# The gate projection by seven products, another order of the seven, and an earlier start of ACT in a two-layer hybrid decoder trunk

## The chip, the cores and the metric

One core of one Trainium2 chip. The time is device microseconds of one execution, the median of 3 runs. Five engines work beside each other, each through its own list of instructions in order: PE (matrix products; PEld is its loading of weights), DVE (elementwise), ACT (elementwise with function tables), POOL (elementwise) and SP, which here only issues transfers from memory. They wait for each other through semaphores.

## The reference

Two layers over 512 tokens of width 1024, all float32, then a last RMSNorm. In each layer the part that this change touches is the feed-forward:

```python
def swiglu(h, w_gate, w_up, w_down):
    return (jax.nn.silu(h @ w_gate) * (h @ w_up)) @ w_down
# in each layer: h = h + hybrid_mixer(rmsnorm(h, ...), w_in, ...)
#                h = h + swiglu(rmsnorm(h, norm_ffn), w_gate, w_up, w_down)
# h: 512 x 1024, w_gate and w_up: 1024 x 2816, w_down: 2816 x 1024
```

The mixer ahead of it (one input projection, dilated attention, Mamba-2 scan, one output projection) is as before, but for the very first product of layer 0: it multiplies the normalised x by 512 columns of w_in.

## The kernel before, in words

The kernel keeps everything transposed: channels on the 128 partitions, the 512 tokens along the free side. hT[0] to hT[7] hold the residual stream.

**Products at full accuracy.** Every float32 operand is split in two fp32r parts, high and low: ACT casts the high part, DVE subtracts to get the low one (split_x for activations, split_w for weights). A product is three matmuls: high x high, high x low, low x high. The split weights live in rings of three buffers each (tags whi and wlo, NWH = 3), each of 128 x 1024: eight 128x128 blocks. Raw weights arrive in chunks of 1 MB in two buffers (tag raw, NRAW = 2): 1024 rows by 256 columns, so two blocks of output channels, a pair.

**The feed-forward.** Its 22 blocks of 128 hidden channels are done in four parts of 6, 6, 6 and 4 (PARTS), so 3, 3, 3 and 2 pairs. A part makes its gate and up blocks, and then its share of the down projection, which adds to hT block by block (eight blocks of 6 x 3 matmuls in a part of six). In the first part of each layer gate and up are plain: block() issues 8 x 3 matmuls of 512 columns for each block. In the other three parts (eight pairs in each layer) the gate blocks are plain and the up pair goes through seven() (line 1114).

**seven().** It computes a 2 x 2 block product (two halves of the 1024 channels, two blocks of outputs, two halves of the 512 tokens) with seven half-size products in place of eight, after Strassen and Winograd. The weight sides of the seven are: two quarters of the raw chunk as they are (tile a, products a0 and aK), one more quarter (tile d, half a buffer), and four sums of quarters, s[0] to s[3], that DVE makes in a tile called wsum (two buffers): s[0] and s[1] are split into tile b, s[2] and s[3] into tile c. Each product is 4 x 3 matmuls of 256 columns. The activation sides (X: b, t12, t34) are made once for a layer in normed(). Before, the seven run in the order a0, aK, bK, b0, c0, cK, d; all four sums are written before b is split, and as the planner counts dependences by tile, the split of b waits for the last of them. DVE (and one copy on ACT) recombine the products in PSUM into two outputs, m and o.

**Who sets the order.** Operations are collected in a Plan with a cost and a due time (at(...), clock[0]), and Plan.schedule places them on the engines by due time, as buffers allow; the result is a fixed list of instructions for each engine. `LEAD` = 14 lets splits and sums be placed up to 14 us ahead of their first product.

**The start (from line 468).** SP issues pmix (8 KB of norm weights), then hT[0], w0[0], hT[1], w0[1] and so on. PE multiplies a tile of ones nine times meanwhile. For each k, ACT scales hT[k] (xh), squares hT[k] for the norm, and casts w0[k]; DVE makes the low parts. ACT's first instruction is a load of its function table, placed behind its wait for hT[0].

Of the kernel before, what the change touches and what calls it, by code (L numbers as in the profile page):

```python
# [15 lines left out]
ALU = mybir.AluOpType  # L16
# [24 lines left out]
E_XW = 'dve'  # L41
RES_G = 6
NEAR_G = 6.0
GATE7 = 0
PARTS = (6, 6, 6, 4)
HH = S // 2
KQ = KD // 2
# [132 lines left out]
class VTile:  # L180


    def __init__(self, pool, shape, dtype, tag, name, space):
        self.pool, self.shape, self.dtype, self.tag, self.name = pool, shape, dtype, tag, name
        self.psum = space
        self.ap = None
        self.writer, self.readers, self.uses = None, [], 0
        self.live = False

    def get(self):  # L190
        if self.ap is None:
            kw = {} if self.tag is None else {"tag": self.tag[0], "bufs": self.tag[1]}
            self.ap = self.pool.tile(self.shape, self.dtype, name=self.name, **kw)
        return self.ap


class Op:
# [6 lines left out]
class Plan:  # L204
# [4 lines left out]
    def add(self, eng, dur, outs, ins, fn, prio=None, table=None, lat=0.0):  # L209
        o = Op()  # L210
        o.eng, o.dur, o.lat, o.fn, o.table = eng, dur, lat, fn, table
        o.prio = self.t if prio is None else prio
        o.n, o.users = len(self.ops), []
        deps = set()
        outs = [v.tile for v in outs]
        ins = [v.tile for v in ins if isinstance(v, View)]
        for t in ins:
            assert t.writer is not None, f"{t.name} is read before it is written"
            deps.add(t.writer)
        for t in outs:  # L220
            if t.writer is not None:
                deps.add(t.writer)
            deps.update(t.readers)
        for t in ins:
            t.readers.append(o)
        for t in outs:
            t.writer, t.readers = o, []
        deps.discard(o)
        o.tiles = list({id(t): t for t in outs + ins}.values())
        for t in o.tiles:  # L230
            t.uses += 1
        o.deps = deps
        for d in deps:
            d.users.append(o)
        self.ops.append(o)
        return o
# [107 lines left out]
def hybrid_trunk(  # L344
# [24 lines left out]
    def C(shape, name, dt=F32):  # L369
        n = nm(name)  # L370
        return View(VTile(cp, shape, dt, None, n, False), shape)

    def G(name, dt=F32):
        return new(gp, [P, S], dt, ("g", NG), name)

    def big(name, dt=F32):
        return new(wp, [P, 4 * S], dt, ("big", 2), name)
# [13 lines left out]
    def R(v):  # L391
        return v.real() if isinstance(v, View) else v

    def at(t):
        plan.t = t
# [9 lines left out]
    def tt(eng, o, a, b, alu):  # L405
        plan.add(eng, dcost(eng, o, [a, b]), [o], [a, b],
                 lambda: ENG[eng].tensor_tensor(R(o), R(a), R(b), alu))  # L407
# [18 lines left out]
    def memset(eng, o, val):  # L426
        plan.add(eng, 0.1 + 0.9e-3 * o.free, [o], [], lambda: ENG[eng].memset(R(o), val))

    TABLE = {AF.Exp: "exp", AF.Ln: "ln", AF.Silu: "silu", AF.Sin: "silu"}

    def act(o, a, func, scale=None, bias=None, accum=None):
        ptr = [s for s in (scale, bias) if isinstance(s, View)]
        outs = [o] + ([accum] if accum is not None else [])

        def fn():
            kw = {}
            if scale is not None:
                kw["scale"] = R(scale)
            if bias is not None:
                kw["bias"] = R(bias)  # L440
            if accum is not None:
                kw["accum_out"] = R(accum)
            if func == AF.Copy and not kw:
                nc.scalar.copy(R(o), R(a))  # L444
            else:
                nc.scalar.activation(R(o), R(a), func, **kw)  # L446
        cost = 0.83e-3 * o.free + (0.053 if a.tile.psum else 0.093) + 0.093 * len(ptr)
        plan.add("act", cost, outs, [a] + ptr, fn, table=TABLE.get(func))

    def mms(outs, prods, each, prio=None):  # L450

# [7 lines left out]
                    nc.tensor.matmul(R(p[0]), R(p[1]), R(p[2]), start=p[3], stop=p[4])  # L459
        plan.add("pe", each * len(prods), outs, ins, fn, prio, lat=0.08)  # L460

    def load(o, src, kb):
        plan.add("sp", max(0.47, kb / 351.0), [o], [], lambda: nc.sync.dma_start(R(o), src), lat=2.0)

    def tposes(t, parts, name=None):
        mms([t], parts, 0.108)


    at(-40.0)
    pmix = C([P, 16], "pmix")  # L470
    load(pmix, columns[:, PC_MIX:PC_MIX + 16], 8)
    hT = [C([P, S], f"hT{k}") for k in range(KD)]

    raw0 = []
    for k in range(KD):
        load(hT[k], xT[k * P:(k + 1) * P, :], 256)
        raw0.append(G("w0"))
        load(raw0[k], w_in[0, k * P:(k + 1) * P, XBC_COL + 1024:XBC_COL + 1024 + S], 256)
    at(-35.0)
    ones = C([P, P], "ones")  # L480
    memset("pool", ones, 1.0)

    t = tr()
    mms([t], [(t[:, 0:P], ones, ones, True, True)] * 9, 0.43)
    nhalf = C([P, NT], "nhalf")
    memset("pool", nhalf, -0.5)

# [63 lines left out]
    class Norm:  # L551
# [2 lines left out]
        def __init__(self, n):  # L554
            self.n, self.ss, self.row = n, None, None

        def square(self, tl, eng="dve"):
            s = G("sq")
            act(s, tl, AF.Square)
            if self.ss is None:  # L560
                self.ss = s
            else:
                tt(eng, self.ss, self.ss, s, ALU.add)
# [31 lines left out]
    for k in range(KD):  # L595
        at(-20.0 + k)
        xs_next.append(split_x(hT[k], pmix[:, k:k + 1]))
        wh, wl = split_x(raw0[k], None)
        for j, t in enumerate(first):
            js = slice(j * P, (j + 1) * P)  # L600
            xh, xl = xs_next[k]
            mms([t], [(t, wh[:, js], xh, k == 0, False), (t, wh[:, js], xl, False, False),
                      (t, wl[:, js], xh, False, k == KD - 1)], 0.2165, clock[0])
            clock[0] += 3 * 0.2165
        at(-12.0 + k)
        norm_next.square(hT[k])


    at(-12.0)
# [504 lines left out]
    def seven(ids, X):  # L1114
        raw = whl[ids[0]][0]
        q = [[raw[:, j * KQ:(j + 1) * KQ, i * P:(i + 1) * P] for j in range(2)] for i in range(2)]
        at(clock[0] - LEAD)

        def split(src, nk=KD):
            hi, lo = new(wp, [P, 8, P], F32R, ("whi", NWH), "whi"), new(wp, [P, 8, P], F32R, ("wlo", NWH), "wlo")  # L1120
            copy("act", hi[:, 0:nk, :], src)
            tt("dve", lo[:, 0:nk, :], src, hi[:, 0:nk, :].bitcast(F32), ALU.subtract)
            return hi, lo
        a = split(raw[:, :, 0:P])
        sm = big("wsum").rearrange("p (k c) -> p k c", c=P)
        s = [sm[:, i * KQ:(i + 1) * KQ, :] for i in range(4)]
        tt("dve", s[0], q[1][0], q[1][1], ALU.add)
        tt("dve", s[1], s[0], q[0][0], ALU.add)
        tt("dve", s[2], q[0][0], q[1][0], ALU.add)
        tt("dve", s[3], q[0][1], s[1], ALU.add)  # L1130
        b = split(sm[:, 0:KD, :])
        c = split(sm[:, KD:, :])
        d = split(q[1][1], KQ)
        t1_, t2_ = slice(0, HH), slice(HH, S)

        def prod(o, w, k0, xs, half):
            hi, lo = w
            for ka in range(0, KQ, 2):
                pr = []
                for k in (ka, ka + 1):  # L1140
                    xh, xl = (v[:, half] for v in xs[k])
                    for i, (wv, v) in enumerate(((hi, xh), (hi, xl), (lo, xh))):
                        pr.append((o, wv[:, k0 + k, :], v, k == 0 and i == 0, k == KQ - 1 and i == 2))
                mms([o], pr, 0.1175, clock[0])
                clock[0] += len(pr) * 0.1175
            at(clock[0] - 6.0)

        def bcast(v):
            return v.unsqueeze(1).broadcast_to([P, 2, HH])

        def halves(v):
            return v.rearrange("p (u c) -> p u c", u=2)

        b1, b2 = X["b"][0:KQ], X["b"][KQ:]
        p17, p26 = hold(), acc()
        e, m, o = G("e"), G("m"), G("o")
        prod(p17[:, 0:HH], a, 0, b1, t1_)
        copy("act", e[:, 0:HH], p17[:, 0:HH])
        prod(p26[:, 0:HH], a, KQ, b2, t1_)
        prod(p26[:, HH:], b, KQ, X["t12"], t2_)  # L1160
        tt("dve", halves(m), halves(p26), bcast(e[:, 0:HH]), ALU.add)
        p45, p3 = acc(), tr()
        prod(p45[:, HH:], b, 0, X["t12"], t1_)
        prod(p17[:, HH:], c, 0, X["t34"], t1_)
        tt("dve", e[:, HH:], p17[:, HH:], m[:, HH:], ALU.add)
        prod(p3[:, 0:HH], c, KQ, b2, t2_)
        tt("dve", m[:, HH:], m[:, HH:], p3[:, 0:HH], ALU.add)
        tt("dve", m[:, HH:], m[:, HH:], p45[:, HH:], ALU.add)
        prod(p45[:, 0:HH], d, 0, X["t34"], t2_)
        tt("dve", halves(o), halves(p45), bcast(e[:, HH:]), ALU.add)  # L1170
        at(clock[0] - 4.0)
        return m, o

# [100 lines left out]
```

## Time and profile before

| | us |
|---|---|
| median of 3 runs | 1323.34 (1321.87 to 1323.98) |
| the profiled execution | 1324.0 |
| its span, first to last instruction | 1322.2 |
| PE busy in the span | 1294.6 (98%) |
| DVE busy | 905.7 (68%) |
| ACT busy | 653.0 (49%) |
| POOL busy | 140.2 (11%) |
| mean granted clock of PE | 0.995 |

The profiled execution gives durations; its own time is 1.8 us above its span and 0.7 us above the median of the runs. Busy shares are means over stages of different kinds: attention and scan keep DVE, ACT and POOL busy, the feed-forward hardly touches POOL. The feed-forward of layer 0 lies at about 275 to 670 us, that of layer 1 at about 928 to 1297 us.

### The profile page before, as it was taken

Reading aid. Unit: us, or ns where it says so; the run is one execution under the profiler, and the core shown is the slowest. Engines: PE = TensorE matmul, PEld = TensorE weight load, DVE = VectorE, ACT = ScalarE, POOL = GpSimd, SP = SyncE. Lnnn points to the kernel's source line nnn. Section 1 sums busy time; section 2 is a strip of 40 time slices with the busy share of each in tenths; the row PEclk is TensorE's granted clock in tenths of the full one; section 3 lists DMA queues with packets and bytes.
Section 4 is the critical chain, followed back from the end, with each engine's and each line's share of the span. In section 5 each row is a group of like instructions: output and inputs, shape, how many; then the busy total and the mean of one; then the engine's idle time right before and its main releaser. Section 6 shows DMA issues by size and latency. Waiting matters only on the chain.

```text
span 1322.2 us, 17020 instructions
## 1 busy us (share of the span) xinstructions
PE 1294.6 (98%) x6674; PEld 1067.4 (81%) x6674; DVE 905.7 (68%) x1510; ACT 653.0 (49%) x1029; POOL 140.2 (11%) x109
## 2 busy tenths in 40 slices
PE   8999998999999999999999999999999999999997
PEld 7877776778888888888888777767888889888896
DVE  6987779768746555555779687887786456465464
ACT  7677656656323323323647687466553233243253
POOL 0014455000000000000000234620000000000000
PEclk9999999999999999999999999999999999999999
DMA  7222211123232233233332222111332332322421
GB/s 242 64 64 64 64 65 64 33 80 102 90 112 96 69 123 99 78 112 96 96 98 65 94 66 65 56 40 45 88 112 84 119 96 72 120 96 73 135 96 63
DMA packets 105727, 115.57 MB, mean 87 GB/s; under 512 B 4656, under 2 KB 95024, under 8 KB 105648
## 3 DMA queue, kind: packets, MB, share of 16 engines
q1 hardware_dynamic: 105648, 114.49, 27.4%
q8 instruction: 52, 0.85, 0.3%
q14 instruction: 27, 0.22, 0.1%
HBM read 112.39 MB, written 2.10 MB: 87 GB/s over the span
## 4 chain that ended last, share of the span: by engine, by line
PE 87%; DVE 7%; ACT 2%; POOL 2%; issue 1%; DMA 0%; POOLq 0%; SPq 0%; DVEq 0%; ACTq 0%
PE acc L459 72%; PE hold L459 7%; PE tr L459 6%; PE tr L457 3%; DVE wlo L407 2%; DVE qs L407 1%; POOL xbc L407 1%; DVE xbc L418 1%; POOL qr L407 1%; ACT whi L444 1%; DVE wsum L407 0%; DVE qs L921 0%; POOL qs L407 0%; ACT L446 0%; DVE sa L413 0%
## 5 line engine op out<-in xcount | busy, mean ns | idle before, releaser
L459 PE MATMUL acc<-xh,whi 128*128 128x512 f32 (+1 forms) x1552 | 588.4, 379 | 1.4 <-DVE o L407 0.9
L459 PE MATMUL acc<-xl,whi 128*128 128x512 f32 (+1 forms) x1552 | 579.4, 373 | 0.0
L459 PE MATMUL acc<-xh,wlo 128*128 128x512 f32 (+1 forms) x1536 | 573.3, 373 | 4.2 <-DVE wlo L407 4.2
L444 ACT CAST whi<-raw 128x1024 fp32r<-128x1024 f32 (+3 forms) x248 | 212.4, 859 | 335.2 <-PE acc L459 303.0
L459 PEld LDWEIGHTS acc<-xh,whi 128*128 128x128 f32 x1552 | 293.2, 189 | 55.1 <-issue 5.6
L459 PEld LDWEIGHTS acc<-xh,wlo 128*128 128x128 f32 x1536 | 289.7, 189 | 58.6 <-DVE wlo L407 6.7
L459 PEld LDWEIGHTS acc<-xl,whi 128*128 128x128 f32 x1552 | 293.3, 189 | 47.1 <-issue 0.5
L407 DVE TENSOR_TENSOR wlo<-raw,whi 128x1024 fp32r<-128x1024 f32 (+2 forms) x240 | 246.8, 1030 | 27.6 <-ACT whi L444 27.3
L407 DVE TENSOR_TENSOR hT<-hT,acc 128x512 f32<-128x512 f32 x104 | 71.1, 685 | 103.6 <-PE acc L459 102.9
L407 DVE TENSOR_TENSOR wlo<-wsum,whi 128x1024 fp32r<-128x1024 f32 x32 | 39.0, 1224 | 88.4 <-ACT whi L444 88.4
L573 POOL TENSOR_TENSOR rcol<-var,nhalf 128x4 f32<-128x4 f32 x8 | 8.7, 1089 | 577.2 <-DVE var L413 577.2
L446 ACT ACT_TABLE_LOAD x49 | 62.9, 1283 | 6.6 <-DMA hT<-in_xT_dram 4.1
L444 ACT CAST whi<-wsum 128x1024 fp32r<-128x1024 f32 x32 | 33.5, 1048 | 53.9 <-PE acc L459 46.3
L418 DVE SCALAR_TENSOR_TENSOR xbc<-cu,prm,xbc 128x511 f32<-128x511 f32 (+2 forms) x72 | 58.4, 819 | 0.8
L444 ACT CAST xh<-ga 128x512 fp32r<-128x512 f32 x44 | 27.3, 621 | 54.5 <-DVE ga L407 38.6
L446 ACT ACTIVATE sa<-sa,mx 128x512 f32<-128x512 f32 (+3 forms) x64 | 36.0, 562 | 36.5 <-DVE mx L979 36.2
L1230 POOL TENSOR_TENSOR fr<-fvar,nhalf 128x1 f32<-128x1 f32 x4 | 2.2, 546 | 353.5 <-DVE fvar L413 353.5
L979 DVE CUSTOM_DVE_ANT_0 sa<-tr,cst 128x512 f32<-128x512 f32 (+3 forms) x64 | 30.7, 479 | 10.3 <-PE tr L459 10.2
L459 PE MATMUL hold<-xh,wlo 128*128 128x256 f32 x128 | 36.3, 284 | 0.0
L459 PE MATMUL hold<-xl,whi 128*128 128x256 f32 x128 | 36.2, 283 | 0.0
L459 PE MATMUL hold<-xh,whi 128*128 128x256 f32 x128 | 36.1, 282 | 0.0
L407 DVE TENSOR_TENSOR xl<-ga,xh 128x512 fp32r<-128x512 f32 x44 | 30.3, 688 | 8.3 <-ACT xh L444 8.2
(216 smaller groups left out, 1654.8 us busy)
## 6 DMA issues: line engine op xcount, KB each, us to landing
raw<-in_w_in_dram SPq DMA_DIRECT2D x24, 1024.0 KB, 5.1
raw<-in_w_gate_dram SPq DMA_DIRECT2D x22, 1024.0 KB, 5.2
raw<-in_w_up_dram SPq DMA_DIRECT2D x22, 1024.0 KB, 5.2
raw<-in_w_down_dram SPq DMA_DIRECT2D x24, 768.0 KB, 4.5
raw<-in_w_out_dram SPq DMA_DIRECT2D x8, 1024.0 KB, 5.0
raw<-in_w_out_dram SPq DMA_DIRECT2D x8, 512.0 KB, 6.3
hT<-in_xT_dram SPq DMA_DIRECT2D x8, 256.0 KB, 5.3
w<-in_w_in_dram SPq DMA_DIRECT2D x8, 256.0 KB, 5.4
```

The source lines that it names most:

```text
L407: lambda: ENG[eng].tensor_tensor(R(o), R(a), R(b), alu))
L418: lambda: nc.vector.scalar_tensor_tensor(R(o), R(a), R(s), R(b), op0, op1))
L444: nc.scalar.copy(R(o), R(a))
L446: nc.scalar.activation(R(o), R(a), func, **kw)
L457: nc.tensor.transpose(R(p[0]), R(p[1]), R(p[2]))
L459: nc.tensor.matmul(R(p[0]), R(p[1]), R(p[2]), start=p[3], stop=p[4])
L573: lambda: nc.gpsimd.tensor_tensor(R(self.r), R(v), R(nhalf), ALU.pow))
L979: nc.vector.tensor_tensor_reduce(R(sa[:, 0:nk]), R(t[:, 0:nk]), R(cst[:, C_MASK + S - nk:C_MASK + S]), 1.0, 3e38, ALU.add, ALU.min, R(m))
L1230: lambda r=r, v=v: nc.gpsimd.tensor_tensor(R(r), R(v), R(nhalf[:, 0:1]), ALU.pow))
```

## The change

GATE7 goes from 0 to 1: seven_gate (line 1055) is then true for every pair of the three later parts, so the gate pair too goes through seven(), with SiLU applied to its outputs (the code for it was there). In seven() the tile d is split right behind a; s[0] and s[1] are one tile of dependences and s[2], s[3] another (class Part), so that b can be split before s[2] and s[3] are made; the order of products becomes a0, aK, d, bK, b0, c0, cK, and the output o is made before the last product. At the start the transfer of hT[0] is issued ahead of pmix, that of w0[0] from ACT's queue, ACT does one square of a column of ones (which brings its table load there), the squares of hT come behind the high part of hT three tiles on, and PE multiplies ones ten times.

```diff
-GATE7 = 0
+GATE7 = 1
...
+class Part:
+    def __init__(self, view):
+        self.view, self.root = view, view.tile
+        self.pool, self.tag, self.name, self.psum = None, None, view.tile.name, view.tile.psum
+        self.writer, self.readers = None, []
+    def get(self):
+        return self.view.real()
...
-    def act(o, a, func, scale=None, bias=None, accum=None):
+    def act(o, a, func, scale=None, bias=None, accum=None, after=()):
...
-    def load(o, src, kb):
+    def load(o, src, kb, eng="sp"):
...
     at(-40.0)
+    ones = C([P, P], "ones")
+    memset("pool", ones, 1.0)
     pmix = C([P, 16], "pmix")
-    load(pmix, columns[:, PC_MIX:PC_MIX + 16], 8)
     for k in range(KD):
         load(hT[k], xT[k * P:(k + 1) * P, :], 256)
+        if k == 0:
+            load(pmix, columns[:, PC_MIX:PC_MIX + 16], 8)
         raw0.append(G("w0"))
-        load(raw0[k], ..., 256)
+        load(raw0[k], ..., 256, "sp" if k else "act")
+    warm = small([P, 1], "warm", 1)
+    act(warm, ones[:, 0:1], AF.Square)
...
-    mms([t], [(t[:, 0:P], ones, ones, True, True)] * 9, 0.43)
+    mms([t], [(t[:, 0:P], ones, ones, True, True)] * 10, 0.43)
...
+    for k in range(KD):
         at(-12.0 + k)
-        norm_next.square(hT[k])
+        norm_next.square(hT[k], after=[xs_next[min(k + 3, KD - 1)][0]])
...
         a = split(raw[:, :, 0:P])
+        d = split(q[1][1], KQ)
         sm = big("wsum").rearrange("p (k c) -> p k c", c=P)
-        s = [sm[:, i * KQ:(i + 1) * KQ, :] for i in range(4)]
+        sums = [part(sm[:, 0:KD, :]), part(sm[:, KD:, :])]
+        s = [sums[i // 2][:, i % 2 * KQ:(i % 2 + 1) * KQ, :] for i in range(4)]
         tt("dve", s[0], q[1][0], q[1][1], ALU.add)
         tt("dve", s[1], s[0], q[0][0], ALU.add)
+        b = split(sums[0])
         tt("dve", s[2], q[0][0], q[1][0], ALU.add)
         tt("dve", s[3], q[0][1], s[1], ALU.add)
-        b = split(sm[:, 0:KD, :])
-        c = split(sm[:, KD:, :])
-        d = split(q[1][1], KQ)
+        c = split(sums[1])
...
-        p17, p26 = hold(), acc()
+        p17, p26, p45, p3 = hold(), acc(), acc(), tr()
         prod(p17[:, 0:HH], a, 0, b1, t1_)
         copy("act", e[:, 0:HH], p17[:, 0:HH])
         prod(p26[:, 0:HH], a, KQ, b2, t1_)
+        prod(p45[:, 0:HH], d, 0, X["t34"], t2_)
         prod(p26[:, HH:], b, KQ, X["t12"], t2_)
         tt("dve", halves(m), halves(p26), bcast(e[:, 0:HH]), ALU.add)
-        p45, p3 = acc(), tr()
         prod(p45[:, HH:], b, 0, X["t12"], t1_)
         prod(p17[:, HH:], c, 0, X["t34"], t1_)
         tt("dve", e[:, HH:], p17[:, HH:], m[:, HH:], ALU.add)
+        tt("dve", halves(o), halves(p45), bcast(e[:, HH:]), ALU.add)
+        tt("dve", m[:, HH:], m[:, HH:], p45[:, HH:], ALU.add)
         prod(p3[:, 0:HH], c, KQ, b2, t2_)
         tt("dve", m[:, HH:], m[:, HH:], p3[:, 0:HH], ALU.add)
-        tt("dve", m[:, HH:], m[:, HH:], p45[:, HH:], ALU.add)
-        prod(p45[:, 0:HH], d, 0, X["t34"], t2_)
-        tt("dve", halves(o), halves(p45), bcast(e[:, HH:]), ALU.add)
```

## Rows read from the trace of the kernel before

**Rows 1.** The profile page: busy time by engine, then the shares of the chain.
```profile
PE 1294.6 (98%) x6674; PEld 1067.4 (81%) x6674; DVE 905.7 (68%) x1510; ACT 653.0 (49%) x1029; POOL 140.2 (11%) x109
PE 87%; DVE 7%; ACT 2%; POOL 2%; issue 1%; DMA 0%; POOLq 0%; SPq 0%; DVEq 0%; ACTq 0%
```

**Rows 2.** Busy time in stretches: length, PE, PEld, DVE, ACT, POOL, clock, DMA share, GB/s.
```profile
408.60:463.86 55.26, 54.29 (x350) 49.09 (x349) 33.03 (x44) 20.57 (x29) 0.00 (x0) 1.00 0.26 86
```

**Rows 3.** The chain in order of time (start, length): plain blocks, then a half-size product.
```profile
312.17 96.59 PE acc L459 x426
...
418.71 1.44 PE tr L459 x12
```

**Rows 4.** Waits of PE over the whole span: total, times, longest.
```profile
PE acc L459 <- DVE wlo L407: 4.2, 5, 1.3
...
PE acc L459 <- DVE o L407: 0.9, 1, 0.9
```

**Rows 5.** DVE in order of time (start, duration) in a seven of layer 0.
```profile
420.75 0.42 DVE L407 TENSOR_TENSOR m<-m,acc 128x256 f32<-128x256 f32 x1
421.21 0.69 DVE L407 TENSOR_TENSOR ga<-ga,m 128x512 f32<-128x512 f32 x1
421.81 1.22 DVE L407 TENSOR_TENSOR wlo<-raw,whi 128x1024 fp32r<-128x1024 f32 x1
422.95 0.69 DVE L407 TENSOR_TENSOR xl<-ga,xh 128x512 fp32r<-128x512 f32 x1
423.55 0.69 DVE L407 TENSOR_TENSOR wsum<-raw 128x512 f32<-128x512 f32 x1
424.27 0.69 DVE L407 TENSOR_TENSOR wsum<-wsum,raw 128x512 f32<-128x512 f32 x1
```

**Rows 6.** Groups by line and shape: count, busy, mean ns, idle before and what ended it.
```profile
L444 ACT CAST whi<-wsum 128x1024 fp32r<-128x1024 f32 x32 | 33.5, 1048 | 53.9 <-PE acc L459 46.3 <-issue 7.7
...
L407 DVE TENSOR_TENSOR m<-acc,e 128x512 f32<-128x512 f32 x16 | 11.1, 691 | 17.4 <-PE acc L459 17.3
```

**Rows 7.** The same for DVE alone, from 408 to 464 us.
```profile
L407 DVE TENSOR_TENSOR wlo<-wsum,whi 128x1024 fp32r<-128x1024 f32 x6 | 7.3, 1225 | 19.0 <-ACT whi L444 19.0
```

**Rows 8.** The first microseconds in order of time, all engines.
```profile
0.73 0.38 SPq L463 DMA_DIRECT2D pmix<-in_columns_dram  x1
...
0.99 3.73 PE L459 MATMUL tr<-ones 128*128 128x128 f32 x18 [0.99 <-POOL nhalf L427]
1.18 0.42 SPq L463 DMA_DIRECT2D hT<-in_xT_dram  x1
...
4.11 1.28 ACT L446 ACT_TABLE_LOAD   x1 [4.11 <-DMA hT<-in_xT_dram]
...
5.41 0.72 ACT L446 ACTIVATE xh<-hT,pmix 128x512 fp32r<-128x512 f32 x1
...
6.04 0.61 ACT L446 ACTIVATE sq<-hT 128x512 f32<-128x512 f32 x1
...
6.56 0.60 ACT L444 CAST xh<-w 128x512 fp32r<-128x512 f32 x1
...
7.21 0.57 PE L459 MATMUL acc<-xh,xh 128*128 128x512 f32 x1 [2.49 <-ACT xh L444]
```

**Rows 9.** Busy time in single microseconds, columns as in rows 2.
```profile
8.00:9.00 1.00, 1.00 (x4) 0.81 (x4) 1.00 (x2) 1.00 (x3) 0.00 (x0) 0.50 1.01 373
```

**Rows 10.** The chain in its first 12 us.
```profile
1.18 2.87 DMA hT<-in_xT_dram
...
7.21 2.80 PE acc L459 x6
10.01 1.85 PE hold L459 x6
```

**Rows 11.** DVE behind the first product, in order of time, with its idle time.
```profile
31.72 0.16 DVE L413 TENSOR_SCALAR var<-tr 128x4 f32<-128x4 f32 x1 [1.74 <-PE tr L459]
34.64 1.29 DVE L407 TENSOR_TENSOR cu<-acc,rstd 128x512 f32<-128x512 f32 x2 [2.76 <-ACT rstd L444]
```

More of the change, by code (lines that the diff above doesn't have):

```diff
@@ L186, in __init__ @@
         self.ap = None
+        self.root = self
         self.writer, self.readers, self.uses = None, [], 0
@@ L194, in get, with part @@
         return self.ap
+class Part:
[5 more added lines that the diff above has]
+        return self.view.real()
+def part(view):
+    return View(Part(view), view.shape)
 class Op:
@@ L228, in add @@
         deps.discard(o)
-        o.tiles = list({id(t): t for t in outs + ins}.values())
+        o.tiles = list({id(t.root): t.root for t in outs + ins}.values())
         for t in o.tiles:
@@ L447, in act @@
         cost = 0.83e-3 * o.free + (0.053 if a.tile.psum else 0.093) + 0.093 * len(ptr)
-        plan.add("act", cost, outs, [a] + ptr, fn, table=TABLE.get(func))
+        plan.add("act", cost, outs, [a] + ptr + list(after), fn, table=TABLE.get(func))
     def mms(outs, prods, each, prio=None):
@@ L460, in mms @@
         plan.add("pe", each * len(prods), outs, ins, fn, prio, lat=0.08)
-    def load(o, src, kb):
-        plan.add("sp", max(0.47, kb / 351.0), [o], [], lambda: nc.sync.dma_start(R(o), src), lat=2.0)
+    def load(o, src, kb, eng="sp"):
+        plan.add(eng, max(0.47, kb / 351.0), [o], [], lambda: ENG[eng].dma_start(R(o), src), lat=2.0)
     def tposes(t, parts, name=None):
@@ L476, in hybrid_trunk @@
         load(hT[k], xT[k * P:(k + 1) * P, :], 256)
+        if k == 0:
+            load(pmix, columns[:, PC_MIX:PC_MIX + 16], 8)
         raw0.append(G("w0"))
-        load(raw0[k], w_in[0, k * P:(k + 1) * P, XBC_COL + 1024:XBC_COL + 1024 + S], 256)
+        load(raw0[k], w_in[0, k * P:(k + 1) * P, XBC_COL + 1024:XBC_COL + 1024 + S], 256, "sp" if k else "act")
+    warm = small([P, 1], "warm", 1)
+    act(warm, ones[:, 0:1], AF.Square)
     at(-35.0)
-    ones = C([P, P], "ones")
-    memset("pool", ones, 1.0)
     t = tr()
-    mms([t], [(t[:, 0:P], ones, ones, True, True)] * 9, 0.43)
+    mms([t], [(t[:, 0:P], ones, ones, True, True)] * 10, 0.43)
     nhalf = C([P, NT], "nhalf")
@@ L555, in __init__, with square @@
             self.n, self.ss, self.row = n, None, None
-        def square(self, tl, eng="dve"):
+        def square(self, tl, eng="dve", after=()):
             s = G("sq")
-            act(s, tl, AF.Square)
+            act(s, tl, AF.Square, after=after)
             if self.ss is None:
```

## The prediction

> **What bounds the kernel now.** I read the page's busy shares first, then the chain, then the stretches of the feed-forward, and DVE's and PE's own order inside them. PE is busy 98% of the span, DVE 68%, ACT 49%, and PE's work is 87% of the chain that ended last [rows 1]: a gain must come from fewer or faster matmuls, or from time in which PE stands still. In a part of the feed-forward with plain gate and seven-product up, PE is busy 54.29 of 55.26 us, DVE only 33.03, ACT 20.57 [rows 2]. All through the kernel PE's largest waits on DVE in the feed-forward are 4.2 us for low weights and 0.9 us for a recombination [rows 4], so some 5 us are lost there, and DVE looks as if it had room. Its order shows why that is only half true: of its idle time in 408 to 464 us, 19.0 us stand before six subtractions on wsum, waiting for ACT's cast [rows 7]; the cast itself waits mostly for PE (46.3 of its 53.9 us) to let go of one of the three weight buffers [rows 6]. DVE is idle because its list is fixed and its next entry can't start.
>
> **PE's work.** Plain blocks run at 96.59 / 426 = 0.2267 us a matmul of 512 columns, half-size products at 1.44 / 12 = 0.1200 us a matmul of 256 [rows 3]. A plain gate pair is 2 x 8 x 3 = 48 matmuls, 10.88 us; a seven is 7 x 4 x 3 = 84, 10.08 us. Saved: 0.80 us a pair. Later parts have 3 + 3 + 2 pairs in each of two layers, 16 in all (the 16 recombinations m of the up pairs confirm it, [rows 6]): 12.8 us.
>
> The Trainium skill has a rule for this spacing (TensorE: Matmul & The Clock Gate, "Back-to-back issue gap"): columns over 2.4 GHz and 2.5 ns. By it a pair would go from 10.36 to 9.17 us and the sixteen would give 19.0 us. The trace disagrees: its two spacings leave some 13 ns beyond the columns for each matmul at either size, a charge that the change pays 84 times in place of 48. The rows are this kernel's own, so the rule gets no chance of its own.
>
> **What it costs on DVE.** Start to start, DVE takes 1.14 us for a subtraction of 1024, 0.60 us for one of 512, 0.72 us where the next reads its result, and 0.46 us for a half-size recombination with such a pause [rows 5]. A seven needs three splits of 1024 and one of 512 (4.02), four sums (3 x 0.60 + 0.72 = 2.52) and two full and three half recombinations (1.20 + 1.38 = 2.58): 9.12 us. A plain gate pair needs two splits, 2.28. The end of a pair (two products, two low parts of activations) is 4 x 0.60 = 2.40. So a pair's DVE work goes from 2.28 + 9.12 + 2.40 = 13.8 us beside 20.96 us of PE to 2 x 9.12 + 2.40 = 20.6 us beside 20.16. Without the pauses of 0.12 (four a seven) it would be 19.7. This is the heart of the case: DVE becomes as long as PE.
>
> Over a part of three pairs DVE has 61.9 us to do and PE 60.5, but not all of DVE's must fall inside. The sums of the first two sevens (5.0 us) can be made under the previous down projection, and the last recombinations and products (some 4 us) finish under the next one. That leaves 53 us in 60.5. What decides is whether each split comes in time. PE's new cycle is a (24 matmuls, to 2.88 us), d (12, to 4.32), b (24, to 7.20), c (24, to 10.08). With three buffers taken in turn, b takes the one that the last c left at 0 and is due at 4.32; c takes a's at 2.88, due at 7.20; the next a takes d's at 4.32, due at 10.08; the next d takes b's at 7.20, due at 12.96. A large split is a cast of 1.05 [rows 6] and a subtraction of 1.22 [rows 5], about 2.3 us, so b and c have 2.0 us to spare and a 3.4. DVE may be that late before PE waits, and the recombinations, which nothing needs at once, can be the ones that lag. So I expect stalls of the kind there is now, for twice as many sevens: 5.1 us [rows 4] become 7.6. From below: the new order removes even today's, -5.1 us; from above: DVE's 20.6 sets the pace and today's kind stays, 0.48 x 16 = +7.7. I take +2.5, between them, nearer to the row of today's stalls.
>
> ACT gets 1.5 more casts and a copy for each gate pair, under 3 us by the cast of 1.05 [rows 6] in a stretch where it is busy 20.57 of 55.26 us [rows 2]: hidden. A SiLU now waits for DVE's recombination m or o, and the casts of the next weights stand behind it on ACT; with DVE late, that hands the lateness on, and it is part of the upper bound. Transfers don't grow in number or size. A raw chunk of the gate is held a little longer, until its sums are made, and the next but one is issued on SP only then; at this point of the cycle PE has over a seven of work left. PSUM takes two buffers more for gate products in place of the two accumulators of plain blocks: nothing. At the end of layer 1 the 16 half-token weight splits of the finish fall on a DVE with no room; I leave 0 for that within a bound of +2 us, an estimate of three or four subtractions of 0.60 that come late.
>
> **The start.** Now hT[0] is issued at 1.18 us and lands 2.87 later [rows 8, 10]; ACT loads its table from 4.11 for 1.28, scales at 5.41, squares at 6.04 and casts w at 6.56; PE starts at 7.21, having stood 2.49 us [rows 8], and then runs at a granted clock of 0.50, its 1.2 GHz level [rows 9]: its first twelve matmuls take 2.80 + 1.85 = 4.65 us [rows 10] in place of 12 x 0.2267 = 2.72.
>
> After: hT[0] takes pmix's slot at 0.73 and lands at 3.60. The table load goes under that wait (w0[0]'s issue and the load end near 2.5). ACT scales at 3.65 and, with the square gone from between, casts 0.63 later and feeds PE 0.65 after that, at 4.93. The ten products of ones run to 0.99 + 10/9 x 3.73 = 5.13, which is then the last to come. So PE starts 2.08 us earlier; and with no idle time ahead of it I expect it not to fall to the 1.2 GHz level, another 1.93. Together 4.0. Against that: pmix now lands behind two transfers of 256 KB, and scaling needs it; and the low part of w0 may be late for the third matmul. If pmix comes over 0.2 us late, PE stands, and if the clock falls for it, the 1.93 is lost. I take 3.3, bounds 1.5 and 4.0. Every further load on SP moves up by one slot (0.45). The squares come later on ACT; their sum isn't needed before PE's first phase ends. Is the gain kept? DVE stands 1.74 us before the norm's variance and 2.76 before the first scaling [rows 11], so it can follow a PE that comes up to 4 us earlier, and its own work moves forward by over 1 us too. I expect it to be kept whole.
>
> **Sum.** -12.8 + 2.5 + 0 - 3.3 = -13.6 us against the profiled execution's 1324.0: 1310.4, and as the median of the runs lies 0.7 lower, **1310 us**.
>
> **The rivals.**
> First, PE alone sets the pace: the new order removes today's waits and the start gives all of its 4.0: 12.8 + 5.1 + 4.0 = 21.9 us, about 1302. For it: DVE's spare 2 us for each split, and d put where its sums aren't needed. Against it: 20.6 us of DVE work beside 20.16. 12%.
>
> Second, DVE sets the pace of the later parts: 20.6 us a pair and today's stalls give 12.8 - 7.7 = 5.1, with the start 8.4, 1315; with another 0.25 us of waiting inside each of 32 sevens all of it goes, 1323. Centre 1318. For it: the sums above; against it: the 9 us of a part's work that lie outside. 20%.
>
> Third, slower: DVE's fixed list blocks itself as in rows 7. If, of the more than 3 us that it now stands before each of those six subtractions, 0.75 us can't be filled in each seven, then with DVE full a pair takes 20.6 + 1.5 = 22.1 against today's 20.96 + 5.1 / 16 = 21.3: 0.8 x 16 = 13 us lost, with the start 9 to 10 lost, 1333. It decides from 21.5 us a pair on. Against it: those waits end with PE's release of a buffer, so they are mostly PE's own pace. 10%.
>
> That the change doesn't do what it says can be only at the start: if the clock falls all the same, it gives 1.5 and the sum is 1312, inside the forecast's own span of 1304 to 1315, which has 58%.
>
> **How the numbers follow.** About 0.2% (2.6 us) is what a measurement of this kernel can tell. Faster by more: 58% + 12% + 14% of the second rival's 20% = 84%. Within: 6%, its rest. Slower: 10%. The range leaves out the third rival and the ends of the first and second: 1303 to 1321.
>
> **What would show it.** Right: the first real matmul near 5.1 us with a granted clock of 1.00 from there; a stretch of the later parts with DVE busy over 90% and PE over 97%; 32 recombinations m, and 768 plain matmuls fewer. Wrong: waits of PE on wlo of over 12 us in total, or PE under 95% in those stretches while DVE has no idle time (second rival), or DVE idle before wlo for several us a seven while PE waits too (third). A first phase at a clock of 0.50 would take 2 us off the start's part.

## The result, and the profile after

The changed kernel takes 1302.56 us (median of 4 runs, 1300.04 to 1303.0), the kernel before beside it 1323.66 (4 runs, 1321.87 to 1326.15): a ratio of 0.9831, with a 95% interval of 0.9809 to 0.9852. That is 21.1 us less. The forecast was 13.3 less (1310), with a range from 1303: the direction came out, the size did not, by 0.4 us past the range's end. The sum is that of the first rival, in which PE alone sets the pace (1302), but not by that rival's terms, as the account below shows.

The profiled execution took 1302.14 us, of which the span is 1300.3. The page first: busy time and the shares of the chain, to be read against [rows 1].

```profile
PE 1280.3 (98%) x7252; PEld 1085.9 (84%) x7252; DVE 1000.5 (77%) x1686; ACT 683.7 (53%) x1078; POOL 141.1 (11%) x109
...
PE 90%; DVE 5%; POOL 2%; ACT 2%; issue 1%; DMA 0%; POOLq 0%; ACTq 0%
```

PE's share of the chain went from 87 to 90%, DVE's from 7 to 5%, although DVE is 95 us longer busy. PE has 578 more records: the sixteen pairs add 16 x (84 - 48) = 576, the tenth product of ones two. More and smaller matmuls: the busy time of PE fell by 14.3.

Where the time went is read from the chain of waits, which has the same pieces at the layers' landmarks in both kernels (start, length).

```profile
275.89 31.51 PE acc L476 x138
311.51 85.71 PE acc L476 x378
...
412.21 4.32 PE acc L476 x36
421.57 5.76 PE acc L476 x48
...
661.92 22.70 PE acc L476 x100
...
916.86 31.51 PE acc L476 x138
...
1291.98 3.17 issue
```

The same four landmarks of the kernel before:

```profile
276.55 31.51 PE acc L459 x138
...
673.48 22.70 PE acc L459 x100
...
928.39 31.51 PE acc L459 x138
...
1313.92 3.16 issue
```

The feed-forward of layer 0 runs from the first piece to the x100, that of layer 1 from the second x138 to the last issue. Layer 0: 673.48 - 276.55 = 396.93 before, 661.92 - 275.89 = 386.03 after. Layer 1: 385.53 before, 375.12 after. So the two feed-forwards give 10.9 and 10.4, together 21.3, and everything before the first of them only 0.7 in this execution. The spacing of the matmuls is as it was [rows 3]: 85.71 / 378 = 0.2267 us, 5.76 / 48 = 0.1200.

Two stretches of later parts after the change (length, then busy time of PE, PEld, DVE, ACT, POOL, clock, DMA share, GB/s), one in each layer, to set beside [rows 2]:

```profile
399.43:459.91 60.48, 60.48 (x500) 60.18 (x499) 54.54 (x80) 29.85 (x40) 0.00 (x0) 1.00 0.29 93
1133.60:1194.10 60.50, 60.50 (x500) 60.20 (x499) 52.53 (x77) 29.91 (x40) 0.00 (x0) 1.00 0.29 95
```

PE has no idle time at all there. DVE is busy 54.5 of 60.5 us; the prediction's count was 53. In the stretch that answers to [rows 7], 408 to 464 us, DVE's low parts of the sums (count, busy, mean ns, idle before and what ended it):

```profile
L424 DVE TENSOR_TENSOR wlo<-wsum,whi 128x1024 fp32r<-128x1024 f32 x10 | 12.2, 1220 | 0.5 <-ACT whi L461 0.5
```

Ten subtractions now follow 0.5 us of idle time; before, six followed 19.0 us. The waits of PE on DVE's wlo and o [rows 4] have no row left in the changed kernel.

### The profile page after: what moved, and what is told of

The parts are those of the page before. It is cut to its first block, busy times and chain, and to the rows that moved or that the text cites. A ratio compares the mean times of both kernels' runs of the same rounds, so it can differ in the third digit from the quotient of the medians.

```text
span 1300.3 us, 18525 instructions
## 1 busy us (share of the span) xinstructions
PE 1280.3 (98%) x7252; PEld 1085.9 (84%) x7252; DVE 1000.5 (77%) x1686; ACT 683.7 (53%) x1078; POOL 141.1 (11%) x109
## 4 chain that ended last, share of the span: by engine, by line
PE 90%; DVE 5%; POOL 2%; ACT 2%; issue 1%; DMA 0%; POOLq 0%; ACTq 0%
PE acc L476 68%; PE hold L476 11%; PE tr L476 8%; PE tr L474 3%; DVE wlo L424 1%; DVE qs L424 1%; POOL xbc L424 1%; DVE xbc L435 1%; POOL qr L424 0%; DMA w<-in_w_in_dram 0%; DVE sa L430 0%; DVE sa L1001 0%; POOL sq L424 0%; POOL qs L424 0%; ACT sa L463 0%
## 5 line engine op out<-in xcount | busy, mean ns | idle before, releaser
L476 PE MATMUL acc<-xh,wlo 128*128 128x512 f32 (+1 forms) x1536 | 545.4, 355 | 0.0
L424 DVE TENSOR_TENSOR wlo<-raw,whi 128x1024 fp32r<-128x1024 f32 (+2 forms) x240 | 237.0, 993 | 17.8 <-ACT whi L461 17.5
L461 ACT CAST whi<-wsum 128x1024 fp32r<-128x1024 f32 x64 | 67.2, 1050 | 84.9 <-PE tr L476 31.1
L424 DVE TENSOR_TENSOR wlo<-wsum,whi 128x1024 fp32r<-128x1024 f32 x64 | 78.2, 1221 | 14.6 <-ACT whi L461 14.3
L476 PE MATMUL hold<-xh,whi 128*128 128x256 f32 x256 | 72.5, 283 | 0.0
L476 PE MATMUL hold<-xh,wlo 128*128 128x256 f32 x256 | 72.5, 283 | 0.0
L476 PE MATMUL hold<-xl,whi 128*128 128x256 f32 x256 | 72.4, 283 | 0.0
L476 PEld LDWEIGHTS hold<-xh,whi 128*128 128x128 f32 x256 | 49.1, 192 | 0.5
L476 PEld LDWEIGHTS hold<-xl,whi 128*128 128x128 f32 x256 | 49.1, 192 | 0.5
L476 PEld LDWEIGHTS hold<-xh,wlo 128*128 128x128 f32 x256 | 49.1, 192 | 0.0
L424 DVE TENSOR_TENSOR wsum<-raw 128x512 f32<-128x512 f32 x64 | 42.2, 685 | 0.3
```

## The experiments

All are compared with the kernel before on the same chip in the same session. The prediction's two open places are whether DVE's work costs PE anything, and what the start gives.

**1. The start alone**: GATE7 is 0 and seven() is as before, only the start is new.

```diff
-GATE7 = 1
+GATE7 = 0
...
-        d = split(q[1][1], KQ)
...
-        prod(p45[:, 0:HH], d, 0, X["t34"], t2_)
...
+        prod(p45[:, 0:HH], d, 0, X["t34"], t2_)
+        tt("dve", halves(o), halves(p45), bcast(e[:, HH:]), ALU.add)
```

> The kernel before with the new start alone (plain gate, old seven). Theory S1, read from the trace after: the start is worth 0.7 us, because ACT begins when hT[0] and w0[0] land together near 4.6 us and PE runs its first dozen matmuls at the 1.2 GHz level again: 1322.9 against 1323.6, not to be told from no change. Rival S2: the level of the clock in those microseconds differs from run to run, and in other executions the start gives 2 to 3 us: 1320 to 1321, with the first dozen matmuls at 0.23 us each in the profile.

1323.06 against 1324.38 us, ratio 0.9985 [0.9971, 1.0]: the start is worth 1.3 to 2 us, with an interval from nothing to 3.8. The feed-forwards are as before (396.60 and 385.75), so that lengths read from single profiles repeat here to about 0.3 us. So about 19 of the 21 us are the gate and the order of the seven.

**2 and 3. The gate with the old seven, and the new seven without the gate.** Run 2 has run 1's seven() and leaves GATE7 at 1; run 3 is the changed kernel with one line changed:

```diff
-GATE7 = 1
+GATE7 = 0
```

> The kernel after with the old order inside a seven (products a0, aK, bK, b0, c0, cK, d, and the split of b waiting for all four sums). Theory O1 (the new order is what takes PE's waits away): the gate still saves 12.8 us of PE's work, but with d last the waits on split weights come twice as often as before: 10 us or more of waits in the later parts, 1312 to 1316. Rival O2 (one seven behind another is smooth by itself; today's waits came from plain gate blocks and sevens taking turns in three buffers): waits under 2 us, 1302 to 1305.

> The kernel after with a plain gate (new order of the seven for the up pairs only, new start). O1: the new order alone removes the 5 to 8 us in which PE stood or ran unevenly in the later parts: 1315 to 1318. O2: the waits stay as plain blocks and sevens still take turns: 1321 to 1323, PE waits on low weights of 3 us or more.

The gate with the old seven: 1324.84 us, 0.9999 [0.9986, 1.0011]. The new seven without the gate: 1316.97, 0.9942 [0.9922, 0.9962]. With the landmarks as above, the sums of both feed-forwards make a table of two by two:

| | old seven | new seven |
|---|---|---|
| plain gate | 782.5 (before) | 774.2 (run 3) |
| gate by seven products | 782.8 (run 2) | 761.2 (after) |

(Run 2: 676.51 - 278.20 = 398.31 and 1318.54 - 934.05 = 384.49. Run 3: 669.59 - 277.03 = 392.56 and 1310.59 - 928.97 = 381.62.) With the old seven the gate gains nothing: what it saves on PE is lost again in standing. The new seven alone gains 8.3, more than the 5.1 of waits in [rows 4], because PE's matmuls also stood apart where no wait is booked: the stretch of [rows 2] holds 110 plain and 240 half-size matmuls, 53.7 us by the spacings of [rows 3], and lasts 55.26, so 1.5 us are lost where its busy time shows 0.97 idle. On the new seven the gate gains 13.0, and PE's saving was worked out as 12.8. The two edits are worth more together than apart: the gate needs the order.

What the old seven does under the gate stands in run 2's rows: a stretch of its later parts (columns as above), then the waits of PE from 395 to 650 us (total, times, longest).

```profile
401.50:466.00 64.50, 61.06 (x494) 59.85 (x493) 54.82 (x79) 29.08 (x40) 0.00 (x0) 1.00 0.29 91
```

```profile
PE acc L476 <- DVE m L424: 5.6, 5, 1.1
PE acc L476 <- DVE wlo L424: 3.0, 5, 0.6
PE acc L476 <- DVE o L424: 0.9, 1, 0.9
```

DVE's busy time is the same as after the change (54.82 against 54.54), but PE stands. In order of time on DVE, one such place (start, duration, idle before):

```profile
425.14 1.23 DVE L424 TENSOR_TENSOR wlo<-wsum,whi 128x1024 fp32r<-128x1024 f32 x1 [0.77 <-ACT whi L461]
...
434.09 0.68 DVE L424 TENSOR_TENSOR m<-acc,e 128x512 f32<-128x512 f32 x1
434.81 0.42 DVE L424 TENSOR_TENSOR e<-hold,m 128x256 f32<-128x256 f32 x1
435.26 0.42 DVE L424 TENSOR_TENSOR m<-m,tr 128x256 f32<-128x256 f32 x1
435.72 0.42 DVE L424 TENSOR_TENSOR m<-m,acc 128x256 f32<-128x256 f32 x1
```

The chain goes on with PE:

```profile
436.19 4.58 PE acc L476 x36
```

From 425.14 to 436.14 DVE has no hole; splits, sums and recombinations stand in one bunch, and PE, having stood 1.12 us, starts again at 436.19, once the last m has given back its accumulator. The work is not too much for DVE, it comes too late.

**4. Another division into parts**: the part of four blocks comes first, so that it is the plain one.

```diff
-PARTS = (6, 6, 6, 4)
+PARTS = (4, 6, 6, 6)
```

> The kernel after with parts of 4, 6, 6 and 6 blocks in place of 6, 6, 6 and 4: the first, plain part is one pair shorter, so one more pair of each layer goes by sevens. Theory P1 (PE alone sets the pace there, DVE has a tenth of its time left): another pair by sevens saves twice 0.80 for gate and up in each layer, 3.2 us in all: 1299.4. Rival P2: the activation sides of the seven, which DVE makes under the first part's down projection, have only two thirds of it left and come late: PE waits 3 us or more in each layer and the time is 1303 or above.

1299.68 us, 0.9809 [0.979, 0.9828]; the changed kernel has 0.9831. It is the lowest time here, though 0.2% below the changed kernel is not clear of noise. One pair more in each layer goes by sevens, expected to give 1.6 each. The profiled span is 3.2 us shorter, the total as expected, but not its places: from layer to layer it takes 913.37 - 275.76 = 637.61 us against 640.97 (3.4 less), and layer 1's feed-forward takes 375.65 against 375.12. Why the last layer gains nothing was not settled; its only PE wait there is one of 1.4 us on wlo, and the chain just ahead of that wait passes through a transfer of a raw chunk (7.47 us from 1087.88), as the changed kernel's does not.

**5 and 6. The order of splits against the order of products.** Run 5 keeps the new splits (a, d, b, c) with the old products (first diff), run 6 the old splits with the new products (second).

```diff
-        prod(p45[:, 0:HH], d, 0, X["t34"], t2_)
         prod(p26[:, HH:], b, KQ, X["t12"], t2_)
...
-        tt("dve", halves(o), halves(p45), bcast(e[:, HH:]), ALU.add)
-        tt("dve", m[:, HH:], m[:, HH:], p45[:, HH:], ALU.add)
         prod(p3[:, 0:HH], c, KQ, b2, t2_)
         tt("dve", m[:, HH:], m[:, HH:], p3[:, 0:HH], ALU.add)
+        tt("dve", m[:, HH:], m[:, HH:], p45[:, HH:], ALU.add)
+        prod(p45[:, 0:HH], d, 0, X["t34"], t2_)
+        tt("dve", halves(o), halves(p45), bcast(e[:, HH:]), ALU.add)
```

```diff
-        d = split(q[1][1], KQ)
...
-        b = split(sums[0])
         tt("dve", s[2], q[0][0], q[1][0], ALU.add)
         tt("dve", s[3], q[0][1], s[1], ALU.add)
-        c = split(sums[1])
+        b = split(sm[:, 0:KD, :])
+        c = split(sm[:, KD:, :])
+        d = split(q[1][1], KQ)
```

> The kernel after (gate by sevens) with the new splits (d behind a; b split as soon as its own two sums are there) but the old order of products (d's product last, o made behind it). Theory B1 (the sums held up the split of b): this half carries most of the 22 us between the all-old order with the gate (1324.8) and after: 1303 to 1308, waits of PE on split weights under 2 us. Rival B2 (the tail of a seven, where o and both last additions come only behind the last product and meet the end of the pair on DVE): still 1315 to 1325, with waits of PE on m and o.

> The kernel after with the old splits (four sums, then b, c, d, the split of b waiting for the last sum) but the new order of products (d third, o before the last product). B1: 1315 to 1330, as d is now needed earliest and split last. B2: 1303 to 1308.

Run 5: 1348.01 us, 1.0171 [1.0154, 1.0188], slower than the kernel before, which neither theory expected. Run 6: 1313.86, 0.9918 [0.9897, 0.9938]; layer 0's feed-forward takes 386.23 (after: 386.03), layer 1's 385.39 (375.12). Run 5's waits of PE:

```profile
PE acc L476 <- DVE wlo L424: 25.7, 27, 1.2
PE acc L476 <- ACT whi L461: 6.0, 18, 0.4
```

A tile d that is split second but multiplied last keeps one of three weight buffers for nearly the whole seven, so the other splits come late. Run 6 shows what the early split of d is for. Its chain in layer 1 goes through six transfers of raw chunks, three of them here:

```profile
1050.75 6.07 DMA raw<-in_w_gate_dram
...
1062.30 5.14 DMA raw<-in_w_up_dram
...
1082.53 5.95 DMA raw<-in_w_up_dram
```

The waits of SP's queue in 918 to 1310 us, run 6 first, then the changed kernel:

```profile
SPq L480 <- DVE wlo L424: 216.5, 23, 14.3
SPq L480 <- DVE m L424: 115.6, 12, 11.3
```

```profile
SPq L480 <- DVE wlo L424: 266.1, 30, 14.0
SPq L480 <- DVE e L424: 52.9, 5, 10.6
```

With d split last, twelve issues of SP end their wait only at DVE's m, far down in a seven; after the change none does. (The releaser is inferred; the m stands beside d's split in DVE's list, which is what frees the raw chunk.) The chain of the changed kernel passes through no raw transfer.

**7 and 8. More work on DVE, misplaced.** One multiplication of 128x512 that nothing needs, behind c's split; in run 8 three, range(3).

```diff
+        for _ in range(1):
+            tt("dve", spare, cosT, sinT, ALU.mult)
```

> The kernel after with one idle DVE product of 512 columns more in each seven, due with the sums (0.60 us; 32 sevens, 19 us of DVE work). In the parts by sevens DVE is busy 54.5 of 60.5 us, so 1.0 us of each seven is free. Theory V1 (the free time decides, since the planner fills DVE's list without holes): nothing is lost, 1302 to 1304 and PE without gaps. Rival V2 (DVE is at its limit, any lateness of a split reaches PE): each addition delays PE by its own length, 1315 to 1322.

> The same with three idle products in each seven (1.8 us, 0.8 more than is free). V1: the overrun alone shows, less what can be done ahead: about 0.8 us for each of 32 sevens, less 5 us ahead of each of six parts where there is room for it, so 5 to 26 us: 1308 to 1328. V2: 1.8 us for each, 1355 to 1360.

1310.6 us (0.9887 [0.9864, 0.991]) and 1321.81 (0.9977 [0.9962, 0.9992]). They say nothing on the question. As the multiplications depended on nothing in the seven, the plan placed them far ahead (first and last start behind the durations in ns):

```profile
L424 DVE TENSOR_TENSOR spare<-cosT,sinT x32: 673/691/1670, 32.1 to 159.1; 128x512 f32<-128x512 f32 x32
```

All 32 lie before 160 us, in the mixer; run 7's feed-forwards are those of the changed kernel (386.02 and 375.14). Run 8's 96 lie between 32.1 and 330.8 us, ahead of the first seven too.

**9 to 11. More work on DVE, tied to the cycle.** The multiplication now reads e, which each seven writes anew; one, two (range(2)) and three (range(3)) of them in each seven, behind d's product.

```diff
+        for _ in range(1):
+            tt("dve", halves(spare), halves(cosT), bcast(e[:, 0:HH]), ALU.mult)
```

> The kernel after with one idle DVE product of 512 columns more in each seven, which reads the copy that ACT makes of the seven's first product, so that it can't be done ahead as in e7 and e8. DVE has 54.5 of 60.5 us in a part of three pairs, 1.0 us free a seven. V1 (the free time decides): 0.60 fits, the feed-forward of each layer is as long as after, to 1 us. V2 (any lateness reaches PE): 0.60 x 16 = 9.6 us more in each layer.

> The same with two (1.2 us, 0.2 more than is free). V1: up to 0.2 x 16 = 3 us more in each layer, and waits of PE begin. V2: 19 us more in each layer.

> The same with three (1.8 us, 0.8 more than is free). V1: 0.8 x 16 = 13 us more in each layer less some us done ahead of each part, 1315 to 1330, and DVE busy over 95% of those parts. V2: 29 us more in each layer, 1355 to 1362.

| more on DVE in each seven | us | ratio to before | layer 0 | layer 1 |
|---|---|---|---|---|
| none (after) | 1302.56 | 0.9831 [0.9809, 0.9852] | 386.03 | 375.12 |
| 0.60 | 1303.4 | 0.9843 [0.9802, 0.9885] | 386.97 | 375.40 |
| 1.20 | 1312.79 | 0.9909 [0.9882, 0.9937] | 389.74 | 381.47 |
| 1.80 | 1320.7 | 0.9962 [0.995, 0.9973] | 395.33 | 383.57 |

The same microseconds of layer 0 in the three runs:

```profile
399.40:459.90 60.50, 60.37 (x497) 59.84 (x496) 58.26 (x87) 30.12 (x40) 0.00 (x0) 1.00 0.26 80
```

```profile
399.40:459.90 60.50, 59.77 (x488) 58.78 (x488) 59.31 (x90) 28.04 (x38) 0.00 (x0) 1.00 0.27 86
```

```profile
399.40:459.90 60.50, 58.81 (x482) 57.86 (x481) 59.95 (x90) 27.02 (x36) 0.00 (x0) 1.00 0.25 81
```

These windows lie 1.3 to 2.2 us later in the feed-forward than the changed kernel's, as the three runs reach it earlier. Laid over the same work as there, DVE is busy 57.3, 58.3 and 58.9 of 60.5 us, against 54.5. One more costs the feed-forwards 1.2 us, two 10.1, three 17.8. The free time of the changed kernel is (60.48 - 54.54) / 6 = 1.0 us a seven, and the price begins between 0.60 and 1.20. That is the limit theory's point. Its size for two was too small (up to 3 us a layer expected, 3.7 and 6.4 measured). In layer 1 part of the price is another wait: the chains of runs 10 and 11 pass there through a raw transfer (5.96 us from 1262.85, 5.24 from 1268.90), and PE's longest wait, 3.3 and 3.0 us, is for the cast behind it; run 11's chain has such a transfer in layer 0 too (7.82 us from 571.78). Whether the place of the added work in DVE's list counts beside its length was not tried.

**12. w0[0] on SP's queue again**, behind hT[0] and pmix, in one execution.

```diff
-        load(raw0[k], ..., 256, "sp" if k else "act")
+        load(raw0[k], ..., 256, "sp")
```

> The kernel after with the transfer of w0[0] on SP, third behind hT[0] and pmix. Theory T1 (two transfers of 256 KB issued together share the DMA engines, so hT[0] lands near 4.6 us and not at 3.6): hT[0] now lands by 3.8 us and ACT starts on it, but w0[0] lands near 4.9, and PE starts at 5.7 to 6.2, no earlier than after. Rival T2 (the 2.9 us that hT[0] took in the trace before were not of sharing): hT[0] lands at 4.4 or later all the same.

1306.28 us, which says nothing of a us or two; the rows do. First the changed kernel's start (start, duration, idle before), then this run's.

```profile
0.73 0.40 ACTq L480 DMA_DIRECT2D w<-in_w_in_dram  x1
0.73 0.38 SPq L480 DMA_DIRECT2D hT<-in_xT_dram  x1
0.99 4.64 PE L476 MATMUL tr<-ones 128*128 128x128 f32 x20 [0.99 <-POOL nhalf L444]
1.17 1.28 ACT L463 ACT_TABLE_LOAD   x1 [1.17 <-PEq L1279]
4.61 0.62 ACT L461 CAST xh<-w 128x512 fp32r<-128x512 f32 x1 [1.95 <-DMA w<-in_w_in_dram]
5.14 1.33 ACT L463 ACTIVATE xh<-hT,pmix 128x512 fp32r<-128x512 f32 x2
5.91 0.79 PE L476 MATMUL acc<-xh,xh 128*128 128x512 f32 x1 [0.28 <-ACT xh L463]
```

```profile
3.67 0.72 ACT L463 ACTIVATE xh<-hT,pmix 128x512 fp32r<-128x512 f32 x1 [1.44 <-DMA pmix<-in_columns_dram]
5.88 0.62 ACT L461 CAST xh<-w 128x512 fp32r<-128x512 f32 x1 [1.49 <-DMA w<-in_w_in_dram]
6.55 0.50 PE L476 MATMUL acc<-xh,xh 128*128 128x512 f32 x1 [0.93 <-ACT xh L461]
```

Issued 0.9 us ahead of w0[0], hT[0] lands after 2.7 us and pmix after 2.4, and ACT scales at 3.67, which is where the prediction put it (3.65). Issued together with w0[0], hT[0] takes 3.7 us, pmix 3.6, and ACT's first real work is at 4.61, the cast of w0[0]. On the one queue w0[0] comes later still, at 5.9 and not near 4.9 as expected, and PE starts at 6.55 instead of 5.91. So the two transfers beside each other cost the first 1.0 us and still win 0.6 for PE. The Trainium skill says as much (DMA: Bandwidth & Descriptors, "Issuing engines are not separate DMA queues"): transfers started by different engines run on the same DMA engines and interleave, and only issue time is saved.

**13 and 14. Which half of the product order counts.** Run 13 keeps d third (and split second) and makes the outputs behind the last product; run 14 makes the outputs ahead of the last product, but splits d last and multiplies it sixth. The diffs stand in this order.

```diff
-        tt("dve", halves(o), halves(p45), bcast(e[:, HH:]), ALU.add)
-        tt("dve", m[:, HH:], m[:, HH:], p45[:, HH:], ALU.add)
         prod(p3[:, 0:HH], c, KQ, b2, t2_)
         tt("dve", m[:, HH:], m[:, HH:], p3[:, 0:HH], ALU.add)
+        tt("dve", m[:, HH:], m[:, HH:], p45[:, HH:], ALU.add)
+        tt("dve", halves(o), halves(p45), bcast(e[:, HH:]), ALU.add)
```

```diff
-        d = split(q[1][1], KQ)
...
         c = split(sums[1])
+        d = split(q[1][1], KQ)
...
-        prod(p45[:, 0:HH], d, 0, X["t34"], t2_)
...
         tt("dve", e[:, HH:], p17[:, HH:], m[:, HH:], ALU.add)
+        prod(p45[:, 0:HH], d, 0, X["t34"], t2_)
         tt("dve", halves(o), halves(p45), bcast(e[:, HH:]), ALU.add)
```

> The changed kernel with d third as there, but m's last sum and the output o made behind the last product cK, as before. Theory P1 (d third is what counts: it gives PE 12 matmuls, 1.44 us, that need no sum of DVE, so b's split may come that much later): as the changed kernel within 2 us, 1301 to 1305, no PE wait on wlo or m over 0.5 us in the feed-forward. Theory P2 (o and m ahead of the last product are what counts: the accumulator of p45 comes free 1.44 us earlier): layer 0's feed-forward goes from 386.0 back towards the 398.3 of the old seven, at least 4 us longer in each layer, so 1310 or more, with PE waits on DVE's m or o.

> The changed kernel with o and m's last sum ahead of the last product as there, but d's product sixth (a0, aK, bK, b0, c0, d, cK) and d split behind c, so that the ring's order and the products' agree. P1 (d third is what counts): b is due 1.44 us earlier in each seven, PE waits on wlo as in the old seven, layer 0's feed-forward at least 4 us over 386.0, time 1310 or more. P2 (o and m early are what counts): layer 0 within 1 us of 386.0; layer 1 may lose up to 10 us as in the run with the old order of splits, where the raw chunk was also held until d's split at the end.

Run 13: 1305.06 us beside 1327.37 for the kernel before on this chip, 0.9834 [0.981, 0.9857]. Run 14: 1310.69, 0.9882 [0.9858, 0.9906].

| seven under the gate | layer 0 | layer 1 |
|---|---|---|
| old (run 2) | 398.3 | 384.5 |
| d third, outputs last (13) | 388.8 | 375.0 |
| d sixth and split last, outputs early (14) | 386.0 | 380.4 |
| d third but split last, outputs early (6) | 386.2 | 385.4 |
| both, d split second (after) | 386.0 | 375.1 |

Neither theory holds as it stood, since either half alone does most of it in layer 0: of 12.3 us, early outputs alone bring all, d third alone 9.5 (PE then waits 1.8 us in four places for m). In layer 1 what counts is that d is split early: 375 where it is, 380 to 385 where it is split last; the chains of run 14 and run 2 there pass through a raw transfer too (5.33 us at 1256.97, 5.36 at 1275.19). Why only layer 1 needs it was not tried; layer 0's chain has no raw transfer in run 14.

## Why the prediction was wrong, point by point

**The step that failed is the stalls**: "So I expect stalls of the kind there is now, for twice as many sevens: 5.1 us become 7.6." It took +2.5. The feed-forwards gave 21.3 us, PE's work 12.8 of it, so the stalls' term was -8.5: past even the prediction's lower bound of -5.1. Three errors lie in it. The stalls of today were scaled up by the number of sevens while the same change rewrote the order that made them; run 2 shows that scaling would have been right with the old order, and by more: its feed-forwards take 21.6 us above the changed kernel's, where before 8.5 were lost (21.3 - 12.8). The size has no source either: twice as many sevens would make 10.2 of 5.1, and 7.6 is half as much again, a point picked between two bounds. And the lower bound counted only the waits that the profile books on DVE, while the new order without the gate gave 8.3.

The prediction had the argument for the other outcome in hand: it counted 53 us of DVE's work in 60.5 and gave the splits of b and c 2.0 us to spare. Both came true (54.5; the limit at 0.6 to 1.2 us more a seven). It then gave "DVE becomes as long as PE" more weight than its own count, and left the first rival 12%. That this rival's 1302 is what was measured is partly luck: it adds 12.8, 5.1 and 4.0, and the runs show about 12.8, 8.5 and 0.7 to 2.0, too little at one place and too much at the other.

**PE's work** (-12.8) was right: 13.0 us by the table of two by two, with both spacings unchanged; the up and gate pairs now show 32 recombinations m, busy 21.9 us. The Trainium skill's formula (TensorE: Matmul & The Clock Gate, "Back-to-back issue gap") would have given an estimated 19.0 us; the page gives it for a matmul by itself, and for a stream of matmuls of 512 columns about 131 ns. The 226.7 ns measured here agree with neither, and the measured spacing decides.

**DVE's cost** per seven was right in size, to about an eighth: DVE's busy time rose by 94.8 us, 5.9 for each of sixteen pairs, where the prediction's count makes 20.6 - 13.8 = 6.8. So the second rival (DVE sets the pace, 1318) had a true mechanism at a wrong place: it begins 0.6 to 1.2 us a seven further on, and run 11 (1320.7) is what it looks like. The third rival (DVE's list blocks itself, slower) is what happens in run 5 by another cause: a buffer held by a split that came before its turn.

**The tail** (0) was right within its bound: layer 1's feed-forward gave 10.4, layer 0's 10.9.

**The start** (-3.3, bounds -1.5 and -4.0) was too large: 1.3 to 2 us in run 1's times, 0.7 in the profile after. Its steps on the way to PE failed. hT[0] did not land at 3.60 but at 4.4, beside w0[0]; pmix, which scaling needs and which the prediction named as a risk, landed at 4.8; ACT's list has the cast of w0[0] first; and the products of ones end at 5.63 (0.99 + 4.64), not 5.13. PE starts at 5.91, 1.3 earlier than [rows 8], not 2.1. And the level of the clock is not certain: in the chain of the changed kernel the first six matmuls take as long as in a start at the lower level, and in run 1 they do not.

```profile
0.73 3.86 DMA w<-in_w_in_dram
...
5.91 3.29 PE acc L476 x6
9.20 2.06 PE hold L476 x6
11.26 1.36 PE acc L476 x6
```

```profile
6.60 1.43 PE acc L476 x5
8.03 1.36 PE hold L476 x6
9.39 1.36 PE acc L476 x6
```

After the change the first dozen ends at 11.26, 0.6 us before the 11.86 of the kernel before [rows 10]; in run 1, with the same start, at 9.39. Of fourteen profiles with this start (all but run 12's) the ones of the changed kernel and of run 4 ended late (11.3), the other twelve between 9.4 and 9.7. That lead is kept, as predicted, up to the feed-forward. In the kernel before the granted clock from 200 to 240 us is 0.96; of the profiles with the new start that show 0.96 there too, and no added work ahead of it, the late two begin the feed-forward at 275.76 and 275.89 and six early ones (runs 1, 5, 9, 11, 13, 14) at 273.69 to 274.30, against 276.55 before. So the start gives 0.7 us or 2.2 to 2.9, by which pace the first dozen runs at; where that clock is 0.87 or 0.91 (runs 2, 3, 6 and 10), the feed-forward begins at 274.5 to 278.2.

So the miss is made of -11.0 us at the stalls and about +1.3 to +2.6 at the start, of opposite sign.

## What to carry to other kernels

Work that saves PE time may be put on another engine as long as its busy sum in that stretch, counted from rows, stays under PE's with some margin: here, in layer 0, a DVE busy 90% of the stretch cost nothing, 95% cost 0.9 us, 96% 3.7 and 97% 9.3. Stalls found in a trace belong to the order of work that made them: don't multiply them by a count when the order changes too, ask for each whether its cause is still there. An order of products, an order of splits and a ring of three buffers are one decision: with the gate by sevens the new splits alone made the kernel 1.7% slower than before, the new products alone gained half of what both did.

## What the runs showed of the hardware that was not expected

The granted clock of a stretch does not always tell the pace. Windows of one us at the start, the changed kernel first, then run 1 (PE's count of matmuls stands behind its busy time, the granted clock behind POOL):

```profile
7.00:8.00 1.00, 1.00 (x3) 0.81 (x3) 0.98 (x2) 0.92 (x2) 0.00 (x0) 1.00 1.00 322
```

```profile
7.00:8.00 1.00, 1.00 (x6) 0.82 (x5) 1.00 (x2) 0.95 (x2) 0.00 (x0) 1.00 1.02 303
```

Both rows show 1.00, but the first has three matmuls of 512 columns and the second six; the first's pace (0.43 us apart) is that of the lower level of [rows 9], although PE had stood only 0.28 us ahead of it. Nor did the pause decide: run 5's PE stood 0.48 us ahead of its first matmul and 0.28 ahead of its second, and ran the next ones 0.23 us apart. Kernels with the same start showed either pace, and why was not found. And of two transfers of 256 KB issued at one moment from two queues, one landed 3.7 us and the other 3.86 us later, where one issued 0.46 us ahead of the next took 2.87 [rows 10].
